# Stick-breaking attention weights: from a sum of softplus terms and one exp to sigmoid times a running product of sigmoids

## The chip, the cores and the metric

The kernel runs on one core of one Trainium2 chip. The core has a matrix engine (PE, whose weight loads the profile lists apart as PEld), a vector engine (DVE), a scalar engine for activation functions (ACT), a general engine (POOL) and DMA queues; each engine works through its own queue in order and waits for others on semaphores. PE writes only PSUM, which has eight banks of 128 x 512 fp32 words. The metric is the time of one execution on the device in microseconds (us), the median of several runs.

## The reference

The model is a decoder trunk of two layers on 512 tokens of width 1024. Every layer is an FFN with half weight, a mixer, and another FFN with half weight. The first layer's mixer is a gated linear attention (GLA), the second's is a stick-breaking attention (SB) with 16 heads of 64 channels. The change is in the SB mixer:

```
z = einsum('bhtd,bhsd->bhts', q_blk, k) * scale          # scale = 1/8
mask = s_pos[None, :] < t_pos[:, None]                    # strictly causal
sp = jnp.where(mask, jax.nn.softplus(z), 0.0)
rem = lax.cumsum(sp, axis=3, reverse=True) - sp
weights = jnp.where(mask, jnp.exp(jax.nn.log_sigmoid(z) - rem), 0.0)
o = einsum('bhts,bhsd->bhtd', weights, v)
```

So the weight of key s for query t is sigmoid(z[t,s]) times the product, over all keys u with s < u < t, of sigmoid(-z[t,u]).

## The kernel before, in words

Activations lie in SBUF transposed, channels on the partitions, as eight tiles `xs` of 128 x 512. Every large product is made from split operands: a tile `t` is cut into a rounded part `h` (fp32r, a format that PE takes in one pass) and the rest `l = t - h`, and `mm3` issues three products: h with h, l with h, h with l (line 80 is `mm`, which most of them go through). Weights come by DMA into `raw` tiles; ACT casts them to `wh` (L152), DVE subtracts to get `wl` (L153). A `Feed` object holds all weight products of the kernel as a long list of entries; a stage calls `feed.step` or `feed.halves` to put a few of those products between its own instructions. A half is a quarter of a projection for one tile (6 matmuls of 512 columns or 12 of 256).

The order of the instructions on each engine is the order in which the program writes them, as far as the framework's list scheduler doesn't move one ahead of another whose operands are late by its own model. `tc.issue_after(x)` puts an instruction behind x on the same engine. The helper `act` (L653 to L656) puts an activation behind the last load of ACT's function table, `st["tab"]`; a table load is its own ACT instruction.

The SB stage (`class SB`, its `run` from L1583) loops over s = 0 to 16. Step s makes the weights of head s (`weights_log`), and transposes and uses the weights of head s-1 (`weights`, and after each second head `values`).

- `weights_log` works in three PSUM tiles `ps_z`, numbered by `bk`: query tile 2 (384 columns of keys), query tiles 1 and 0 together (256 and 128 columns in use), query tile 3 (512 columns). For each query tile there are two matmuls, q with `kh` and q with `kl` (L1484 through `logits`). Then a mask product (also L1484, bf16, `ps_z<-negm,idb`) adds -1e30 on and above the diagonal: identity `idb` times a 128 x 128 table `negm`, once for each diagonal block. From step s = 5 on, the mask products of the first two tiles are issued ahead, in the step before (`masks`), and open the accumulation.
- From the masked logits y ACT computes |y| (L1527), exp(-|y|) and ln(1 + that) (both through L656) and relu(y) (L1530). Relu plus logarithm is softplus(y). DVE sums softplus backwards along the keys, one scan for each query tile (L1533), and subtracts: r = y - scan (L1541, reading PSUM), which is the logarithm of the weight.
- `weights` transposes r by PE in 128 x 128 blocks into three `ps_T` tiles (L1555); ACT takes exp on the way to SBUF (`wt`, through L656). Of masked places nothing remains, since exp(-1e30) is 0.
- `values` multiplies with v (L1570, `ps_oT`); ACT and DVE cut the result (L1579, L1580). The output projection (`ps_b`, through L80) starts in the last steps.
- `parts` cuts the next pair of heads' q and k tiles (L1478 on ACT, L1441 and L1464 to L1466 on DVE); its casts are put behind the relu.

PSUM tiles come from four tags: "a" 2 banks, "z" 3, "t" 2, "o" 1. `ps_z` uses "z", `ps_T` uses "t", `ps_oT` uses "o". SBUF buffers `r` are double, `l` single.

At the start of the stage a square root is taken (L578), which needs a function table of its own, and then the table with exp and ln is loaded (L651). That table serves the SB stage and then the normalisation of the FFN behind it (`rstd_wide`, Ln and Exp through L656); only after that is the table for silu loaded (L928).

Of the kernel before, what the change touches and what calls it, by code (L numbers as in the profile page):

```python
# [46 lines left out]
def decoder(ctx: ExitStack, tc: tile.TileContext, a: dict, out: bass.AP):  # L47
# [13 lines left out]
    def psum(name, tag=None):  # L61
        if tag is None:
            tag = order[turn_[0] % 8]
            turn_[0] += 1
        return pp.tile([P, T], F32, tag=tag, bufs=banks[tag], name=name)
# [580 lines left out]
            evac(ps)  # L646
        deferred.clear()

    def exp_ln_tables(after):
        with tc.issue_after(after):  # L650
            st["tab"] = nc.scalar.preload_act_table_set("natural_log_exp_and_others").ins  # L651

    def act(o, i, fn, **kw):  # L653

# [4 lines left out]
    class FFN:  # L659
# [328 lines left out]
        def run(self, between=None):  # L988
            with tc.tile_pool(name="hp", bufs=8, reuse_waits="tile") as self.hp, tc.tile_pool(
                name="tp", bufs=5, reuse_waits="tile"  # L990
            ) as self.tp:
                st["few"] = self.hp
                new_norm()
                if st["ss"] is not None:
                    if self.after_ffn:
                        exp_ln_tables(st["closed"])
                    two_halves(lambda after: sums_wide(self.tp, after))
                    rstd_wide()
                flush(self.defer)
# [24 lines left out]

    class GLA:
# [322 lines left out]
        def run(self):  # L1348
            with ExitStack() as es:
# [10 lines left out]
                stats_a("t")  # L1360
                self.gate_low()
                stats_b("t")
                exp_ln_tables(st["sqrt"])
                flush(self.defer)
                self.gate_logits()
                feed.entries(2)
# [34 lines left out]
    class SB:  # L1401
# [5 lines left out]
        AHEAD = 5  # L1407

        def __init__(self, w_in, w_out, nxt):
            self.defer, self.qk, self.hs = [], {}, []  # L1410
# [72 lines left out]
        def logits(self, o_, l_, r_, first, last=False):  # L1483
            nc.tensor.matmul(o_, l_, r_, start=first, stop=last, skip_group_check=True)  # L1484

        def mask(self, bk, ps, first):

            w = self.WID[bk]
            m0 = P if bk == 2 else w - P
            nb = (w - m0) // P  # L1490
            self.logits(
                ps[:, m0:w].rearrange("p (n s) -> p n s", n=nb),
                self.idb,
                self.negm.unsqueeze(1).to_broadcast([P, nb, P]),
                first,
                not first,
            )

        def masks(self, s):


            if self.AHEAD <= s < 16:
                for bk in (1, 2):
                    self.zs[bk] = psum("ps_z", "z")
                    self.mask(bk, self.zs[bk], True)

        def weights_log(self, p, e):

            m = self.qk[p, e, "q"]
            kh, kl = self.qk[p, e, "k"]  # L1510
            self.ys[p, e] = ys = [None] * 3
            for bk, tiles in ((1, (2,)), (2, (1, 0)), (0, (3,))):
                ahead = bk in self.zs
                ps = self.zs.pop(bk) if ahead else psum("ps_z", "z")
                w = self.WID[bk]
                for n_, i in enumerate(tiles):

                    c0, n = self.BK[i][1], max(2, i + 1) * P
                    ts_ = slice(i * P, (i + 1) * P)
                    o_, h_, l_ = ps[:, c0 : c0 + n], turns(kh)[:, 0 : n // 2], turns(kl)[:, 0 : n // 2]  # L1520
                    self.logits(o_, m[:, ts_], h_, n_ == 0 and not ahead)
                    self.logits(o_, m[:, ts_], l_, False, ahead and i == tiles[-1])
                if not ahead:
                    self.mask(bk, ps, False)
                r = self.hp.tile([P, w], F32, tag=f"r{bk}", name="r")
                l = self.hp.tile([P, w], F32, tag=f"l{bk}", bufs=1, name="l")
                nc.scalar.activation(l, ps[:, 0:w], AF.Abs)  # L1527
                act(l, l, AF.Exp, scale=-1.0)
                act(l, l, AF.Ln, bias=1.0)
                st["relu"] = nc.scalar.activation(r, ps[:, 0:w], AF.Relu).ins  # L1530
                for i in tiles:
                    c = slice(self.BK[i][1], self.BK[i][1] + (i + 1) * P)
                    nc.vector.tensor_tensor_scan(  # L1533
                        out=l[:, c][:, ::-1],
                        data0=r[:, c][:, ::-1],
                        data1=l[:, c][:, ::-1],
                        initial=0.0,
                        op0=ALU.add,
                        op1=ALU.add,
                    )  # L1540
                nc.vector.tensor_tensor(out=r, in0=ps[:, 0:w], in1=l, op=ALU.subtract)  # L1541
                ys[bk] = r
                yield

        def weights(self, p, e):
            ys = self.ys.pop((p, e))
            self.wt[p, e] = wt = []
            for bk, blocks in ((0, (0,)), (1, (1, 3)), (2, (2,))):
                ps = psum("ps_T", "t")
                w = self.TW[bk]  # L1550
                c0 = 0
                for j in blocks:
                    for i in range(j, NT):
                        yb, yc = self.BK[i]
                        nc.tensor.transpose(ps[:, c0 : c0 + P], ys[yb][:, yc + j * P : yc + (j + 1) * P], ident)  # L1555
                        c0 += P
                t = self.hp.tile([P, w], F32, tag=f"w{bk}", name="wt")
                act(t, ps[:, 0:w], AF.Exp)
                wt.append(t)
                yield  # L1560

# [21 lines left out]
        def run(self):  # L1583
            with ExitStack() as es:
# [5 lines left out]
                self.ys, self.wt, self.zs = {}, {}, {}  # L1590
# [10 lines left out]
                exp_ln_tables(st["sqrt"])  # L1601
                flush(self.defer)
                feed.step(4)

# [2 lines left out]
                for s in range(17):  # L1607
                    p, e = divmod(s, 2)
                    q, f = divmod(s - 1, 2)
                    n = steps[s]  # L1610
                    if s < 16:
                        for i, _ in enumerate(self.weights_log(p, e)):
                            if i != 1:
                                self.parts(st["relu"])
                            if i == 1:
                                k = 2 if n > 4 else 1
                                feed.halves(k)
                                n -= k
                    if s > 0:
                        for i, _ in enumerate(self.weights(q, f)):  # L1620
                            if i < 2:
                                k = min(n, n % 2 if i == 0 and n % 2 else 2)
                                feed.halves(k)
                                n -= k
                            if i == 1:
                                self.masks(s + 1)
                        feed.halves(n)
                        if f == 1:
                            self.values(q)
                    else:  # L1630
                        feed.halves(n)
# [368 lines left out]
```

## Time and profile before

| What | Value |
|---|---|
| median of 3 runs | 1758.55 us (1758.52 to 1758.58) |
| the profiled execution's own time | 1758.83 us |
| its span, first to last instruction | 1756.8 us |
| granted TensorE clock, mean | 0.999 |
| busy over the span: PE, PEld, DVE, ACT, POOL | 1744.8, 1627.8, 1508.8, 1065.0, 55.7 us |
| logits of the SB stage on PE | from 1220.5 to 1385.1 us |

How to read it: the page's first part gives the busy time of each engine. Matmuls are pipelined, so the duration that a row gives for one matmul is longer than the time until the next one starts; what a matmul costs PE is read from the distance between starts. In a timeline row stand the start in us, the duration in us, engine, line, operation, output and inputs by the program's names, shape and count, and in brackets how long the engine was idle before and who ended that. In a row of groups the two numbers behind the bar are the union of busy time in us and the mean duration of one instruction in ns; then comes the idle time before them.

### The profile page before, as it was taken

Reading aid. Unit: us, or ns where it says so; the run is one execution under the profiler, and the core shown is the slowest. Engines: PE = TensorE matmul, PEld = TensorE weight load, DVE = VectorE, ACT = ScalarE, POOL = GpSimd, SP = SyncE. Lnnn points to the kernel's source line nnn. Section 1 sums busy time; section 2 is a strip of 40 time slices with the busy share of each in tenths; the row PEclk is TensorE's granted clock in tenths of the full one; section 3 lists DMA queues with packets and bytes.
Section 4 is the critical chain, followed back from the end, with each engine's and each line's share of the span. In section 5 each row is a group of like instructions: output and inputs, shape, how many; then the busy total and the mean of one; then the engine's idle time right before and its main releaser. Section 6 shows DMA issues by size and latency. Waiting matters only on the chain.

```text
span 1756.8 us, 31456 instructions
## 1 busy us (share of the span) xinstructions
PE 1744.8 (99%) x12746; PEld 1627.8 (93%) x12746; DVE 1508.8 (86%) x2490; ACT 1065.0 (61%) x1911; POOL 55.7 (3%) x77
## 2 busy tenths in 40 slices
PE   9999999999999999999999999999999999999998
PEld 8999999889888999999989999999888889999997
DVE  8999797786888999889798988977898679998886
ACT  7556555555655555555656555655888755565555
POOL 0000000200000000000000000010000000000000
PEclk9999999999999999999999999999999999999999
DMA  5533435412123433444434344352212234434441
GB/s 168 156 110 119 130 111 146 118 56 81 57 93 100 132 109 121 120 121 127 128 101 133 103 126 129 106 133 84 85 49 73 73 96 133 123 106 121 120 137 62
DMA packets 186389, 193.16 MB, mean 110 GB/s; under 512 B 4930, under 2 KB 171124, under 8 KB 186244
## 3 DMA queue, kind: packets, MB, share of 16 engines
q1 hardware_dynamic: 177760, 175.91, 32.1%
q0 software_dynamic: 8240, 14.95, 4.7%
q8 instruction: 100, 1.64, 0.4%
q14 instruction: 45, 0.37, 0.1%
q10 hardware_dynamic: 244, 0.29, 0.0%
HBM read 175.17 MB, written 2.10 MB: 101 GB/s over the span
## 4 chain that ended last, share of the span: by engine, by line
PE 90%; DVE 6%; ACT 2%; issue 1%; DMA 1%; DVEq 0%; SPq 0%
PE ps_w L779 21%; PE ps_f L80 15%; PE ps_d L80 15%; PE ps_q L779 10%; PE ps_z L779 5%; PE ps_t L80 5%; PE ps_w L412 5%; PE ps_b L80 4%; PE ps_q L412 2%; DVE wl L153 1%; PE ps_z L1484 1%; PE ps_z L412 1%; PE ps_oT L1570 1%; PE ps_bt L80 1%; PE ps_T L1555 1%
## 5 line engine op out<-in xcount | busy, mean ns | idle before, releaser
L153 DVE TENSOR_TENSOR wl<-raw,wh 128x1024 fp32r<-128x1024 f32 x241 | 255.2, 1059 | 37.4 <-ACT wh L152 36.5
L152 ACT CAST wh<-raw 128x1024 fp32r<-128x1024 f32 x241 | 222.2, 922 | 72.2 <-PE ps_f L80 27.2
L153 DVE TENSOR_TENSOR wl<-s,wh 128x1024 fp32r<-128x1024 f32 x160 | 195.1, 1219 | 66.4 <-ACT wh L152 65.8
L779 PE MATMUL ps_w<-th,wh 128*128 128x256 f32 x864 | 238.9, 277 | 0.3 <-ACT ps_z L807 0.3
L779 PE MATMUL ps_w<-th,wl 128*128 128x256 f32 x864 | 237.6, 275 | 0.0
L779 PE MATMUL ps_w<-tl,wh 128*128 128x256 f32 x864 | 237.6, 275 | 0.0
L152 ACT CAST wh<-s 128x1024 fp32r<-128x1024 f32 x160 | 168.7, 1054 | 6.0 <-DVE s L765 6.0
L779 PEld LDWEIGHTS ps_w<-th,wh 128*128 128x128 f32 x864 | 165.8, 192 | 1.1 <-ACT ps_z L807 0.5
L80 PE MATMUL ps_f<-xh,wh 128*128 128x512 f32 x432 | 166.3, 386 | 0.0
L779 PEld LDWEIGHTS ps_w<-tl,wh 128*128 128x128 f32 x864 | 165.9, 192 | 0.0
L779 PEld LDWEIGHTS ps_w<-th,wl 128*128 128x128 f32 x864 | 165.8, 192 | 0.0
L80 PE MATMUL ps_f<-xh,wl 128*128 128x512 f32 x432 | 164.0, 380 | 0.5 <-DVE wl L153 0.5
L80 PE MATMUL ps_f<-xl,wh 128*128 128x512 f32 x432 | 163.8, 379 | 0.0
L80 PE MATMUL ps_d<-hh,wh 128*128 128x512 f32 x416 | 157.8, 379 | 0.0
L80 PE MATMUL ps_d<-hh,wl 128*128 128x512 f32 x416 | 157.7, 379 | 0.0
L80 PE MATMUL ps_d<-hl,wh 128*128 128x512 f32 x416 | 157.7, 379 | 0.0
L153 DVE TENSOR_TENSOR wl<-rawd,wh 128x1024 fp32r<-128x1024 f32 (+1 forms) x100 | 96.1, 961 | 8.9 <-ACT wh L152 8.8
L807 ACT COPY ps_z<-ps_w 128x256 f32<-128x256 f32 x72 | 26.0, 362 | 118.1 <-PE ps_w L779 117.8
L363 POOL DMA_DIRECT2D x<-d x53 | 46.0, 909 | 1549.3 <-ACT d L362 1091.4
L80 PEld LDWEIGHTS ps_f<-xh,wl 128*128 128x128 f32 x432 | 81.8, 189 | 11.4 <-DVE wl L153 0.9
L80 PEld LDWEIGHTS ps_f<-xl,wh 128*128 128x128 f32 x432 | 81.7, 189 | 11.5
L80 PEld LDWEIGHTS ps_f<-xh,wh 128*128 128x128 f32 x432 | 81.7, 189 | 10.7
(357 smaller groups left out, 5419.2 us busy)
## 6 DMA issues: line engine op xcount, KB each, us to landing
raw<-in_ffn_w_gate_dram SPq DMA_DIRECT2D x43, 1024.0 KB, 5.3
raw<-in_ffn_w_up_dram SPq DMA_DIRECT2D x43, 1024.0 KB, 5.4
rawd<-in_ffn_w_down_dram SPq DMA_DIRECT2D x84, 512.0 KB, 3.8
x<-d POOLq DMA_DIRECT2D x53, 256.0 KB, 4.8
raw<-in_gla_w_in_dram SPq DMA_DIRECT2D x12, 1024.0 KB, 5.3
raw<-in_sb_w_in_dram SPq DMA_DIRECT2D x16, 512.0 KB, 3.8
raw<-in_gla_w_out_dram SPq DMA_DIRECT2D x4, 1024.0 KB, 5.1
raw<-in_sb_w_in_dram SPq DMA_DIRECT2D x4, 1024.0 KB, 5.2
```

The lines of the kernel that those rows point to most:

```text
L80: st["pe"] = nc.tensor.matmul(ps, l, r, start=first, stop=last).ins
L152: nc.scalar.copy(h[:, k], part)
L153: nc.vector.tensor_tensor(out=l[:, k], in0=part, in1=h[:, k].bitcast(F32), op=ALU.subtract)
L363: nc.gpsimd.dma_start(xs[k], d, accum_op=ALU.add)
L412: st["pe"] = nc.tensor.matmul(ps, l_, r_, start=first and c + n == 0, stop=c == 1 and n == 2, skip_group_check=True).ins
L779: st["pe"] = nc.tensor.matmul(o, l_, r_, start=first and j + n == 0, stop=j == 3 and n == 2, skip_group_check=True).ins
L807: v["copied"] = nc.scalar.copy(z, w).ins
L1484: nc.tensor.matmul(o_, l_, r_, start=first, stop=last, skip_group_check=True)
L1555: nc.tensor.transpose(ps[:, c0 : c0 + P], ys[yb][:, yc + j * P : yc + (j + 1) * P], ident)
L1570: nc.tensor.matmul(po[e * 64 : e * 64 + 64, j * P : T], self.v[j][:, c : c + 64], self.wt[p, e][bk][:, c0 : c0 + n], start=j == 0, stop=j ...
```

## The change

The weights are computed as they stand in the last sentence on the reference, without logarithms:

- l = sigmoid(-z) for a whole `ps_z` tile (one activation), r = sigmoid(z) for each query tile by itself, without the query tile's last column (one activation each).
- The scan runs backwards over l with multiply and then add: state = state * l[u] + own[u]. `own` is a new 128 x 512 tile, zero but for an identity in its last 128 columns, so that the state is 0 until the key u = t, is set to 1 there (l[u] is multiplied into a 0), and is from then on the product of sigmoid(-z). This starts each query's product at its own diagonal and so does the masking.
- DVE multiplies r[s] by l[s+1], both in SBUF. The last column of each query tile in r is set to 0 once at the start.
- The mask products, `negm`, `idb`, the list `zs` of tiles opened ahead and `AHEAD` go. The first logit matmul opens the accumulation and the last closes it.
- The exp on the way out of the transposes becomes a copy.
- Buffers: `l` (one for each bk) and `r` (two for each bk, one for even and one for odd heads) are allocated once in the stage's pool; POOL sets `own`'s 384 zero columns and the eight zero columns of r at the start, in place of the DMA of `negm`. DVE copies the identity into `own`, in place of the copy to bf16.
- The table load at the stage's start is that with sigmoid. The FFN behind the stage loads the table with exp and ln again, behind the last sigmoid: one table load more than before.
- The casts in `parts` are put behind the last sigmoid of a tile in place of the relu.

```diff
-    def exp_ln_tables(after):
+    def tables(after, name="natural_log_exp_and_others"):
         with tc.issue_after(after):
-            st["tab"] = nc.scalar.preload_act_table_set("natural_log_exp_and_others").ins
+            st["tab"] = nc.scalar.preload_act_table_set(name).ins
...
                     if self.after_ffn:
-                        exp_ln_tables(st["closed"])
+                        tables(st["closed"])
+                    elif "sigm" in st:
+                        tables(st["sigm"])
...
-                    self.logits(o_, m[:, ts_], h_, n_ == 0 and not ahead)
-                    self.logits(o_, m[:, ts_], l_, False, ahead and i == tiles[-1])
-                if not ahead:
-                    self.mask(bk, ps, False)
-                r = self.hp.tile([P, w], F32, tag=f"r{bk}", name="r")
-                l = self.hp.tile([P, w], F32, tag=f"l{bk}", bufs=1, name="l")
-                nc.scalar.activation(l, ps[:, 0:w], AF.Abs)
-                act(l, l, AF.Exp, scale=-1.0)
-                act(l, l, AF.Ln, bias=1.0)
-                st["relu"] = nc.scalar.activation(r, ps[:, 0:w], AF.Relu).ins
+                    self.logits(o_, m[:, ts_], h_, n_ == 0)
+                    self.logits(o_, m[:, ts_], l_, False, i == tiles[-1])
+                act(l, ps[:, 0:w], AF.Sigmoid, scale=-1.0)
+                for i in tiles:
+                    c = slice(self.BK[i][1], self.BK[i][1] + (i + 1) * P - 1)
+                    act(r[:, c], ps[:, c], AF.Sigmoid)
+                st["sigm"] = st["last"]
                 for i in tiles:
                     c = slice(self.BK[i][1], self.BK[i][1] + (i + 1) * P)
                     nc.vector.tensor_tensor_scan(
                         out=l[:, c][:, ::-1],
-                        data0=r[:, c][:, ::-1],
-                        data1=l[:, c][:, ::-1],
+                        data0=l[:, c][:, ::-1],
+                        data1=self.own[:, T - (i + 1) * P :][:, ::-1],
                         initial=0.0,
-                        op0=ALU.add,
+                        op0=ALU.mult,
                         op1=ALU.add,
                     )
-                nc.vector.tensor_tensor(out=r, in0=ps[:, 0:w], in1=l, op=ALU.subtract)
+                nc.vector.tensor_tensor(out=r[:, 0 : w - 1], in0=r[:, 0 : w - 1], in1=l[:, 1:w], op=ALU.mult)
...
-                act(t, ps[:, 0:w], AF.Exp)
+                nc.scalar.copy(t, ps[:, 0:w])
...
-                self.idb = vp.tile([P, P], BF16, name="idb")
-                self.negm = vp.tile([P, P], BF16, name="negm")
-                nc.vector.tensor_copy(self.idb, ident)
-                nc.gpsimd.dma_start(self.negm, a["c_neg"])
+                self.own = vp.tile([P, T], F32, name="own")
+                nc.gpsimd.memset(self.own[:, 0 : T - P], 0.0)
+                nc.vector.tensor_copy(self.own[:, T - P : T], ident)
...
-                exp_ln_tables(st["sqrt"])
+                tables(st["sqrt"], "sigmoid_and_others")
...
-                                self.parts(st["relu"])
+                                self.parts(st["sigm"])
...
-                            if i == 1:
-                                self.masks(s + 1)
```

More of the change, by code (lines that the diff above doesn't have):

```diff
@@ L1362, in run @@
                 stats_b("t")
-                exp_ln_tables(st["sqrt"])
+                tables(st["sqrt"])
                 flush(self.defer)
@@ L1405, in decoder @@
         TW = (512, 512, 256)
-        AHEAD = 5
         def __init__(self, w_in, w_out, nxt):
@@ L1484, in logits @@
             nc.tensor.matmul(o_, l_, r_, start=first, stop=last, skip_group_check=True)
[L1486 to L1505, printed above, removed]
         def weights_log(self, p, e):
@@ L1512, in weights_log @@
             for bk, tiles in ((1, (2,)), (2, (1, 0)), (0, (3,))):
-                ahead = bk in self.zs
-                ps = self.zs.pop(bk) if ahead else psum("ps_z", "z")
+                ps = psum("ps_z", "z")
                 w = self.WID[bk]
+                r, l = self.r[bk][e], self.l[bk]
                 for n_, i in enumerate(tiles):
@@ L1589, in run @@
                 self.v = [vp.tile([P, D], F32, name=f"w{i}") for i in range(NT)]
-                self.ys, self.wt, self.zs = {}, {}, {}
+                self.ys, self.wt = {}, {}
                 self.later, self.hold = [], False
-                self.idb = vp.tile([P, P], BF16, name="idb")
-                self.negm = vp.tile([P, P], BF16, name="negm")
-                nc.vector.tensor_copy(self.idb, ident)
-                nc.gpsimd.dma_start(self.negm, a["c_neg"])
+                self.own = vp.tile([P, T], F32, name="own")
+                nc.gpsimd.memset(self.own[:, 0 : T - P], 0.0)
+                nc.vector.tensor_copy(self.own[:, T - P : T], ident)
+                self.l = [vp.tile([P, w], F32, name=f"l{bk}") for bk, w in enumerate(self.WID)]
+                self.r = []
+                for bk, w in enumerate(self.WID):
+                    self.r.append([vp.tile([P, w], F32, name=f"r{bk}{e}") for e in range(2)])
+                    for i in range(NT):
+                        if self.BK[i][0] == bk:
+                            c = self.BK[i][1] + (i + 1) * P - 1
+                            for r in self.r[bk]:
+                                nc.gpsimd.memset(r[:, c : c + 1], 0.0)
                 new_norm()
@@ L1600, in run @@
                 stats_b("t")
-                exp_ln_tables(st["sqrt"])
+                tables(st["sqrt"], "sigmoid_and_others")
                 flush(self.defer)
```

## The prediction

> **What bounds the kernel now.** I read the page first, then the busy times of the SB stage by windows, then PE's timeline there, the waits, and the groups of ACT and DVE.
>
> ```profile
> PE 1744.8 (99%) x12746; PEld 1627.8 (93%) x12746; DVE 1508.8 (86%) x2490; ACT 1065.0 (61%) x1911; POOL 55.7 (3%) x77
> PE 90%; DVE 6%; ACT 2%; issue 1%; DMA 1%; DVEq 0%; SPq 0%
> ```
>
> The second line is the chain that ended last, by engine. PE is busy 99% and carries 90% of the chain: what leaves PE's queue shortens the kernel, what leaves another engine counts only where PE waited for it. Two windows show the stage, the stretch with all heads in flight and the whole of it:
>
> ```profile
> core 0: us, PE busy (x) PEld busy (x) DVE busy (x) ACT busy (x) POOL busy (x), PEclk, DMA share, GB/s
> 1250.00:1390.00 140.00, 139.02 (x899) 115.03 (x899) 118.03 (x170) 123.56 (x253) 0.00 (x0) 1.00 0.22 69
> 1216.00:1400.00 184.00, 183.02 (x1162) 152.67 (x1161) 152.59 (x216) 156.06 (x314) 0.00 (x0) 1.00 0.24 74
> ```
>
> The reader is to see three things. PE has no room (183.02 of 184). ACT, light in the rest of the kernel, is at 88% between 1250 and 1390, so here it can be late for PE. DVE is at 84% there, and the change takes little from it. The clock is full and DMA is at a fifth to a quarter, so neither binds.
>
> **Part 1, the mask products: off the path itself.** They are counted in the row of line 1484:
>
> ```profile
> L1484 PE MATMUL ps_z<-negm,idb x48: 230/230/283, 1221.0 to 1385.1; 128*128 128x128 bf16 x32, 128*128 128x256 bf16 x16
> ```
>
> 48 of them, three for each of 16 heads. The 230 ns is not the price, since matmuls overlap; the price is how much later the following products start. There are three positions. First, the masks in line with the logits, as heads 0 to 4 have them in the first two tiles (5 heads); PE's timeline:
>
> ```profile
> 1230.19 0.33 PE L1484 MATMUL ps_z<-kl,mq 128*128 128x384 f32 x1
> 1230.36 0.23 PE L1484 MATMUL ps_z<-negm,idb 128*128 128x128 bf16 x1
> ...
> 1230.59 0.28 PE L1484 MATMUL ps_z<-kl,mq 128*128 128x256 f32 x1
> ...
> 1230.81 0.28 PE L1484 MATMUL ps_z<-kl,mq 128*128 128x256 f32 x1
> 1230.93 0.28 PE L1484 MATMUL ps_z<-negm,idb 128*128 128x256 bf16 x1
> ...
> 1231.27 0.38 PE L80 MATMUL ps_f<-xh,wl 128*128 128x512 f32 x1
> ```
>
> and the same passages in a later head, whose masks were issued ahead:
>
> ```profile
> 1285.98 0.34 PE L1484 MATMUL ps_z<-negm,idb 128*128 128x128 bf16 x2
> 1286.40 0.44 PE L1555 MATMUL ps_T<-ident,r 128*128 128x128 f32 x2
> ...
> 1286.84 0.33 PE L1484 MATMUL ps_z<-kl,mq 128*128 128x384 f32 x1
> ...
> 1287.11 0.28 PE L1484 MATMUL ps_z<-kl,mq 128*128 128x256 f32 x1
> ...
> 1287.34 0.28 PE L1484 MATMUL ps_z<-kl,mq 128*128 128x256 f32 x1
> ...
> 1287.66 0.38 PE L80 MATMUL ps_f<-xh,wl 128*128 128x512 f32 x1
> ```
>
> From `kl` to `kl` it is 1230.59 - 1230.19 = 0.40 us with the mask and 1287.11 - 1286.84 = 0.27 without: 0.13. From the last `kl` to the second weight product it is 1231.27 - 1230.81 = 0.46 with and 1287.66 - 1287.34 = 0.32 without: 0.14. Most of that is not the streaming of the mask but the product behind it, which starts its successor late after a change from bf16. Five heads at 0.27 us: 1.3 us.
>
> Second, the pair issued ahead, between weight products and transposes (heads 5 to 15, 11 heads):
>
> ```profile
> 1274.23 0.38 PE L80 MATMUL ps_f<-xl,wh 128*128 128x512 f32 x1
> 1274.45 0.34 PE L1484 MATMUL ps_z<-negm,idb 128*128 128x128 bf16 x2
> 1274.62 0.38 PE L1555 MATMUL ps_T<-ident,r 128*128 128x128 f32 x2
> ```
>
> Third, the mask of the 512-column tile, between `kl` and transposes (all heads but the first, where a weight product follows it), and a passage into transposes with no mask before it:
>
> ```profile
> 1290.26 0.38 PE L1484 MATMUL ps_z<-kl,mq 128*128 128x512 f32 x1
> 1290.47 0.23 PE L1484 MATMUL ps_z<-negm,idb 128*128 128x128 bf16 x1
> 1290.54 0.61 PE L1555 MATMUL ps_T<-ident,r 128*128 128x128 f32 x4
> ...
> 1292.07 0.38 PE L80 MATMUL ps_f<-xl,wh 128*128 128x512 f32 x1
> 1292.28 0.38 PE L1555 MATMUL ps_T<-ident,r 128*128 128x128 f32 x2
> ```
>
> Without a mask the transposes start 1292.28 - 1292.07 = 0.21 us behind a 512-column product. With the pair it is 1274.62 - 1274.23 = 0.39, with the single mask 1290.54 - 1290.26 = 0.28. So 0.18 for the pair and 0.07 for the single one: 11 x 0.18 = 2.0, 15 x 0.07 = 1.05, and 0.13 for the first head as in the first position. Sum: 1.3 + 2.0 + 1.05 + 0.13 = **4.4 us** (rounded down). Nothing covers it; PE goes straight on to the next product.
>
> **Part 2, ACT's chain.** These groups of the stage (1205 to 1402) are Exp and Ln on SBUF, and Relu from PSUM as the measure for a sigmoid:
>
> ```profile
> L656 ACT ACTIVATE l<-l 128x384 f32<-128x384 f32 x64 | 33.0, 528 | 0.2
> L656 ACT ACTIVATE l<-l 128x512 f32<-128x512 f32 x32 | 20.7, 648 | 0.0
> L1530 ACT ACTIVATE r<-ps_z 128x384 f32<-128x384 f32 x32 | 15.7, 490 | 0.0
> ```
>
> Exp and Ln go: 33.0 + 20.7 = 53.7 us. Abs becomes sigmoid(-z) on the same tile, Relu becomes sigmoid(z); whether a sigmoid takes as long as these no row shows, but exp and relu lie within 40 ns of each other here, so I take the same. Splitting the middle tile adds one instruction a head: between nothing and 0.49 us (the 384-column row), so at most 8 us. ACT's 156 us in 1216 to 1400 fall to about 102 to 110, some 60%. By itself that is worth nothing; it is worth what PE waited for ACT. The waits in the stage (1210 to 1400), of PE's weight loads:
>
> ```profile
> PEld ps_T L1555 <- ACT wt L656: 1.1, 3, 0.6
> PEld ps_b L80 <- DVE r L1541: 0.7, 1, 0.7
> PEld ps_b L80 <- ACT w L1426: 0.5, 1, 0.5
> ```
>
> Together 2.3 us. One of them is the stall in the rows above at 1285.98: the transposes come 0.42 us behind the first mask of the pair, where 1274.62 - 1274.45 = 0.17 is the undisturbed distance. It waits for an exp `wt` that frees the `ps_T` bank, at the end of an ACT backlog. The DVE row is the last head: its weights r hang on abs, exp, ln, scan. All three have ACT's chain behind them, and that chain loses two of four steps. I take **2.0 us**, near the whole, since ACT will have 40% free; the bounds are 0 (DVE takes ACT's place as the late one) and 2.3.
>
> **Part 3, DVE.** The scans stay, the subtraction becomes a product of two SBUF tiles, one column shorter:
>
> ```profile
> L1533 DVE TENSOR_TENSOR_SCAN l<-r,l 128x512 f32<-128x512 f32 x16 | 19.5, 1219 | 4.6 <-ACT l L656 4.5
> L1533 DVE TENSOR_TENSOR_SCAN l<-r,l 128x128 f32<-128x128 f32 x16 | 6.4, 399 | 0.0
> L1541 DVE TENSOR_TENSOR r<-ps_z,l 128x512 f32<-128x512 f32 x16 | 11.0, 691 | 1.0
> L536 DVE TENSOR_TENSOR ss<-ss,sq 128x512 f32<-128x512 f32 x7 | 4.8, 681 | 0.0
> ```
>
> The last row, from behind the stage, has two SBUF inputs: 681 ns against 691 with PSUM, so the product costs what the subtraction did. `ps_z` is free once ACT has read it, earlier than before, as DVE no longer reads it. A scan with multiply and add instead of add and add has no row; I take it as unchanged, the slower case is a rival. Worth 0 either way while DVE stays below PE.
>
> **Part 4, tables and the start.** One table load more, behind the last sigmoid:
>
> ```profile
> L651 ACT ACT_TABLE_LOAD  x3: 1283/1283/1283, 346.2 to 1205.8; - x3
> 1415.21 1.05 ACT L152 CAST wh<-raw 128x1024 fp32r<-128x1024 f32 x1 [7.15 <-PE ps_b L80]
> ...
> 1434.56 0.63 ACT L656 ACTIVATE R<-v 128x512 f32<-128x512 f32 x1
> L1101 POOL MEMSET w<- 128x512 f32 x1 | 1.4, 1355 | 0.0
> ```
>
> 1.28 us on ACT. Queued behind it can be casts of weights (L152), for which DVE and then PE wait; the FFN's Ln, the last row but one, needs it only at 1434.56. ACT idles 7.15 us ahead of 1415.21, and the casts there wait for PE, not for ACT. I take 0; the most it can cost is its own 1.28. [...]
>
> On POOL one DMA issue makes way for nine memsets; by the last row the largest (384 columns) takes about a microsecond. Nothing is queued behind them until the next FFN, and the first multiplication that needs them waits for a head's logits and sigmoids anyway. Worth 0.
>
> **The sum.** 1758.83 (the profiled execution) - 4.4 - 2.0 = 1752.4. The runs' median is 0.28 lower than that execution, so **1752.1 us**, 6.4 us or 0.36% faster. No change means within 0.2%, 3.5 us, about what a measurement of this kernel can tell.
>
> **Rivals.**
> *Masks only.* ACT's relief is not felt, since DVE, still at 84%, is now the late one and PE loses the same 2.0 us to it. For it: DVE has only 16% to spare, and one of the three waits is for DVE. Against it: the other two are for ACT directly, and the idle time ahead of the 512-column scans (4.6 us) ended with ACT (4.5), so DVE itself was fed late. Time 1758.55 - 4.4 = 1754.1.
> *The saving comes smaller than 3.5 us.* The list scheduler places transposes in more and smaller groups once r is ready earlier by its model; each change of format delays the next product as measured above, 0.13 us or so. Some 20 more changes cost 2.6 us, or the table load lands in front of a cast for 1.3. With masks only, 1755.4 to 1756.7.
> *Larger.* If a mask ahead of transposes gave back as much as one ahead of products, 0.27 for a pair and 0.13 for a single one, that would be 11 x 0.09 + 15 x 0.06 = 1.9 us more: 1750.2. The rows of the transposes speak against it.
> *Slower: DVE becomes the bound through the scan.* The scan's pace is (1219 - 399) / 384 = 2.14 ns an element. If a product in the recurrence takes longer than a sum, 1280 elements a head over 16 heads pay. DVE has 184 - 152.6 = 31 us of room, less the 6 us that PE gives up: 25 us, or 1.2 ns an element. Above that PE waits: at double the pace (+2.14 ns, 44 us) DVE is 19 us over, and the time is 1752.1 + 19 = 1771. It decides from about 1.5 ns an element, where the excess eats the gain. [...] No run here shows a scan with a product.
>
> **How the numbers follow.** My forecast 0.62, masks only 0.15, larger 0.08, smaller than 3.5 us 0.10, slower 0.05. The range goes from the larger case with a little margin, 1749.5, to the middle of the smaller case, 1756.0; it leaves out half of the latter, the slower one, and a little at the low end. Faster by over 0.2%: 0.62 + 0.15 + 0.08 = 0.85, less 0.02 for a masks-only case that loses more: 0.83. Within 0.2%: 0.12. Slower: 0.05.
>
> **What would show each step.** Right: in the changed profile no bf16 matmul among the logits; transposes 0.21 us behind the 512-column product before them everywhere; ACT near 60% and DVE still near 84 to 88% in the stage; no wait of PE for `wt` or `r` over 0.2 us; sigmoid rows at 0.49 and 0.61 us, scans at 1.22. The stage, from the first logit matmul to the last `ps_oT`, should be 6 us shorter, and everything behind it shifted by the same amount. Wrong: scans over 1.8 us; waits of PE for DVE l or r in every head; a stage shorter by 6 us with the gain lost behind it at the table load; or ACT as busy as before.

## The result and the profile after

The changed kernel takes 1751.95 us (median of six runs, 1751.57 to 1753.74) against 1758.54 us before (six runs, 1758.42 to 1760.37): a ratio of 0.9963, with a 95% interval from 0.9950 to 0.9976. That is 6.6 us less, where 6.4 were forecast. A second set of runs (e11 below) gave 1751.66 us and a ratio of 0.9961 (0.9948 to 0.9975). The profiled execution took 1752.18 us, its span is 1750.2 us, its granted clock 0.999.

First the page's busy times and its chain by engine:

```profile
PE 1740.0 (99%) x12698; PEld 1628.1 (93%) x12698; DVE 1507.0 (86%) x2490; ACT 1026.3 (59%) x1832; POOL 55.8 (3%) x85
PE 95%; DVE 4%; ACT 1%; issue 0%; DVEq 0%
```

PE has 48 instructions fewer, the mask products, and now carries 95% of the chain instead of 90%. DVE has as many instructions as before and 1.8 us less work. ACT lost 79 instructions and 38.7 us. The same two windows of the SB stage as before:

```profile
1250.00:1390.00 140.00, 139.79 (x886) 119.13 (x885) 117.61 (x171) 94.23 (x189) 0.00 (x0) 1.00 0.22 68
1216.00:1400.00 184.00, 183.76 (x1143) 157.44 (x1142) 155.63 (x225) 121.90 (x241) 0.00 (x0) 1.00 0.24 75
```

The columns are the window, its length, then the busy time of PE, PEld, DVE, ACT and POOL, the clock, the DMA share and GB/s. Between 1250 and 1390 PE now lacks 0.21 us of being busy throughout (0.98 before). ACT fell from 88% to 67%. DVE stays at 84%. What is left of the waits of PE and its weight loads in the stage (1210 to 1400) for another engine, in all:

```profile
PEld ps_b L80 <- ACT w L1426: 0.6, 1, 0.6
PEld ps_T L1531 <- ACT wt L1534: 0.4, 1, 0.4
PE ps_b L80 <- ACT w L1426: 0.2, 1, 0.2
```

The columns are who waited for what, us in all, how often, and the longest. The first and the last are the same place seen from the load and from the product.

Where the time went can be read from the first logit product and the last `ps_oT` of the two kernels. From the view by line, before and then after:

```profile
L1484 PE MATMUL ps_z<-kh,mq x64: 272/356/483, 1220.7 to 1384.6; 128*128 128x256 f32 x32, 128*128 128x384 f32 x16, 128*128 128x512 f32 x16
L1570 PE MATMUL ps_oT<-wt,w x128: 272/432/643, 1251.4 to 1399.2; 128*64 128x512 f32 x32, 128*64 128x384 f32 x32, 128*64 128x256 f32 x32, 128*64 128x128 f32 x32
```

```profile
L1484 PE MATMUL ps_z<-kh,mq x64: 272/301/430, 1221.0 to 1379.4; 128*128 128x256 f32 x32, 128*128 128x384 f32 x16, 128*128 128x512 f32 x16
L1546 PE MATMUL ps_oT<-wt,w x128: 272/433/644, 1250.8 to 1393.3; 128*64 128x512 f32 x32, 128*64 128x384 f32 x32, 128*64 128x256 f32 x32, 128*64 128x128 f32 x32
```

Behind the colon stand the shortest, median and longest duration in ns, then the first and the last start in us. The stage ran from 1220.7 to 1399.2, that is 178.5 us; it now runs from 1221.0 to 1393.3, that is 172.3 us. So 6.2 us of the 6.6 lie in the stage itself. The rest is small and lies outside it: in these two profiles the stage starts 0.3 us later, and some 0.7 us are gained behind it. The SB groups of the changed kernel (1205 to 1402), for ACT and DVE:

```profile
L656 ACT ACTIVATE l<-ps_z 128x384 f32<-128x384 f32 x32 | 15.8, 493 | 5.8 <-PE ps_z L1484 5.5
L656 ACT ACTIVATE r<-ps_z 128x511 f32<-128x511 f32 x16 | 9.7, 604 | 0.0
L1509 DVE TENSOR_TENSOR_SCAN l<-l,own 128x512 f32<-128x512 f32 x16 | 19.4, 1215 | 0.0
L1509 DVE TENSOR_TENSOR_SCAN l<-l,own 128x128 f32<-128x128 f32 x16 | 6.5, 406 | 0.0
L1517 DVE TENSOR_TENSOR r<-r,l 128x511 f32<-128x511 f32 x16 | 11.0, 690 | 1.2
```

A sigmoid takes what an abs or a relu took (0.49 us at 384 columns), the scan with a product what the scan with a sum took (1215 ns against 1219), the product what the subtraction took (690 against 691). And the matmuls at two of the places where masks stood, from PE's timeline:

```profile
1365.72 0.33 PE L1484 MATMUL ps_z<-kl,mq 128*128 128x384 f32 x1
...
1365.99 0.28 PE L1484 MATMUL ps_z<-kl,mq 128*128 128x256 f32 x1
...
1379.64 0.38 PE L1484 MATMUL ps_z<-kl,mq 128*128 128x512 f32 x1
1379.86 0.60 PE L1531 MATMUL ps_T<-ident,r 128*128 128x128 f32 x4
```

From `kl` to `kl` it is 0.27 us, and the transposes start 0.22 us behind the 512-column product: the undisturbed distances of the prediction.

### The profile page after: what moved, and what is told of

The parts are those of the page before. It is cut to its first block, busy times and chain, and to the rows that moved or that the text cites. A ratio compares the mean times of both kernels' runs of the same rounds, so it can differ in the third digit from the quotient of the medians.

```text
span 1750.2 us, 31332 instructions
## 1 busy us (share of the span) xinstructions
PE 1740.0 (99%) x12698; PEld 1628.1 (93%) x12698; DVE 1507.0 (86%) x2490; ACT 1026.3 (59%) x1832; POOL 55.8 (3%) x85
## 4 chain that ended last, share of the span: by engine, by line
PE 95%; DVE 4%; ACT 1%; issue 0%; DVEq 0%
PE ps_w L779 22%; PE ps_f L80 16%; PE ps_d L80 16%; PE ps_q L779 11%; PE ps_z L779 6%; PE ps_w L412 5%; PE ps_t L80 5%; PE ps_b L80 4%; PE ps_q L412 2%; PE ps_z L412 1%; PE ps_z L1484 1%; PE ps_oT L1546 1%; PE ps_T L1531 1%; PE ps_bt L80 1%; PE ps_S L80 1%; PE ps_o L80 1%
```

## The experiments

The theory: PE's path loses 4.4 us of mask products, and some 2 us in which PE waited for ACT. The first rival: masks only, because DVE takes ACT's place as the late engine. The second: DVE, with a scan that could have been slower, is close to binding. Times are medians; the ratio is to the kernel before, timed on the same chip (1758.30 to 1758.55 us).

**e1, the old chain without its masks.** The kernel before, with the mask products left out, so that its weights are not masked:

```diff
-                    self.logits(o_, m[:, ts_], h_, n_ == 0 and not ahead)
-                    self.logits(o_, m[:, ts_], l_, False, ahead and i == tiles[-1])
-                if not ahead:
-                    self.mask(bk, ps, False)
+                    self.logits(o_, m[:, ts_], h_, n_ == 0)
+                    self.logits(o_, m[:, ts_], l_, False, i == tiles[-1])
...
-                            if i == 1:
-                                self.masks(s + 1)
```

> The kernel before without its mask products (so later keys are not masked and the output is not the reference's); the log chain on ACT stays. Theory (two separate gains: 4.4 us of mask products on PE, about 2 us of waits for ACT): 1758.5 - 4.4 = 1754.1 us, and PE's waits for ACT in the stage stay at about 2 us. Rival 1 (the masks carried it all, their place in the queue made the waits): 1752 us, as the changed kernel. Rival 2 (the masks lay in time that PE waited anyway, the gain came from ACT): 1757 us or more, with longer waits for ACT.

**e2, the new chain with the old masks.** The mask products are back at their old places, adding zeros (a table of 0 instead of -1e30):

```diff
+            if self.AHEAD <= s < 16:
+                for bk in (1, 2):
+                    self.zs[bk] = psum("ps_z", "z")
+                    self.mask(bk, self.zs[bk], True)
...
-                    self.logits(o_, m[:, ts_], h_, n_ == 0)
-                    self.logits(o_, m[:, ts_], l_, False, i == tiles[-1])
+                    self.logits(o_, m[:, ts_], h_, n_ == 0 and not ahead)
+                    self.logits(o_, m[:, ts_], l_, False, ahead and i == tiles[-1])
+                if not ahead:
+                    self.mask(bk, ps, False)
...
+                nc.gpsimd.memset(self.negm, 0.0)
```

> The changed kernel with the 48 mask products back in their old three positions, with a table of zeros, so that they add nothing. Theory: 1752.0 + 4.4 = 1756.4 us, and the waits of PE for ACT stay as short as in the changed kernel. Rival 1 (masks carried it all): 1758.5 us. Rival 2 (the gain came from ACT): 1752 to 1754 us.

e1 took 1754.41 us (ratio 0.9978, 0.9969 to 0.9987), e2 1755.86 us (0.9985, 0.9977 to 0.9994). With 1758.36 before (same chip) and 1751.95 after (the first set of runs, with 1758.54 before), the masks are worth 3.95 us on the old chain and 3.9 on the new one, and the chain is worth 2.5 in both cases. Both terms exist: the runs of e1 and e2 (1754.22 to 1757.24) all lie below those of the kernel before and above those of the changed one, so "masks only" is out. Whether the two simply add up, the whole times can't tell; the stage can, and the section on the prediction comes to that. The waits of PE's weight loads in e1 show what ACT's old chain costs once the masks are gone:

```profile
PEld ps_T L1552 <- ACT wt L656: 3.2, 4, 1.1
PEld ps_b L80 <- DVE r L1538: 0.7, 1, 0.7
PEld ps_b L80 <- ACT w L1426: 0.5, 1, 0.5
```

In the kernel before these were 1.1, 0.7 and 0.5 us. Without masks PE reaches the transposes sooner, finds that `wt` has not yet left the bank, and waits 3.2 us there.

**e3, ACT's old load in the new chain.** Two copies of l on itself, between the sigmoid and the scan, in place of exp and ln:

```diff
                 act(l, ps[:, 0:w], AF.Sigmoid, scale=-1.0)
+                act(l, l, AF.Copy)
+                act(l, l, AF.Copy)
```

> The changed kernel with two more copies of l onto itself on ACT behind each sigmoid(-z), where exp and ln stood: the same chain length and nearly the same ACT load as before (about 54 us more). Theory: the waits of PE for ACT come back, 1752.0 + 2 = 1754 us. Rival (the 2 us came from something else, such as DVE not reading PSUM or the order of the queue): 1752 us.

It took 1755.00 us (0.9982, 0.9973 to 0.9991), 3.05 more than the changed kernel, and PE waits as in e1:

```profile
PEld ps_T L1533 <- ACT wt L1536: 3.2, 4, 1.2
```

So ACT's time alone brings the chain's share back, and half a microsecond more. DVE's product still reads only SBUF here, so that its subtraction read PSUM was not what cost the time. What e3 leaves open is how: because the scan gets l later, or because the copies `wt` stand further back in ACT's queue.

**e4, the same load beside the chain.** Two copies of the zero tile `own` into a tile that nobody reads, behind the sigmoids:

```diff
                 st["sigm"] = st["last"]
+                for _ in range(2):
+                    act(self.junk[:, 0:w], self.own[:, 0:w], AF.Copy)
```

> The changed kernel with the same two more ACT copies of each tile's width, but behind the sigmoids and into a scratch tile, so that the chain to the weights is as short as in the changed kernel and only ACT's load is back (about 54 us more). If ACT's backlog makes PE wait (my reading of the wait for wt): 1754 us, as with the copies in the chain. If it is the length of the chain from logits to weights: 1752 us.

It took 1769.37 us (1.0065, 1.0051 to 1.0079), which no theory gave, and the cause lies in the experiment. ACT's timeline and PE's waits:

```profile
1217.87 4.85 ACT L656 ACTIVATE junk<-own 128x512 bf16<-128x512 f32 x8
```

```profile
PE ps_oT L1548 <- ACT wt L1536: 5.7, 6, 1.9
```

The copies depend on nothing in the loop, so the list scheduler pulled them forward in bulk, eight in a row here. They stood ahead of work that PE needed. e4 does not measure what it was meant to.

**e5, the same load, held in its place.** The copies now read `ps`, and each is put behind the tile's last sigmoid:

```diff
                 st["sigm"] = st["last"]
+                with tc.issue_after(st["sigm"]):
+                    for _ in range(2):
+                        nc.scalar.copy(self.junk[:, 0:w], ps[:, 0:w])
```

> The changed kernel with two more ACT copies of each ps_z tile to a scratch tile, this time bound behind the sigmoids of that tile (they read the logits and follow the last sigmoid), so that they can't be drawn forward in a bulk as the free copies were. ACT's load is as before (about 50 us more), the chain from logits to weights stays short. If backlog on ACT makes PE wait: about 1755 us, as with the copies in the chain (1755.0). If the length of the chain does: 1752 us.

It took 1754.29 us (0.9975, 0.9966 to 0.9985): 2.3 of e3's 3.05 us come although the copies no longer stand between a tile's sigmoid and its scan. DVE's rows bear that out: idle time of the scans that ended with l is 10.2 us in e3, 1.0 in e5 and 1.8 in the changed kernel. The largest wait of PE is again the one for `wt`:

```profile
PEld ps_T L1534 <- ACT wt L1537: 3.3, 3, 1.2
```

So most of the chain's worth is the queue ahead of the copies `wt`; up to 0.7 us may be the latency of l, a difference that lies inside the intervals.

**e6 and e7, DVE's room.** One and two more scans of 512 columns for each head, on tiles that nobody reads, behind the last product:

```diff
                 ys[bk] = r
+                for _ in range(1 if bk == 0 else 0):      # e7: 2
+                    with tc.issue_after(made):            # made: the product of L1517
+                        nc.vector.tensor_tensor_scan(
+                            out=self.junk, data0=self.own, data1=self.own, initial=0.0, op0=ALU.mult, op1=ALU.add
+                        )
```

> The changed kernel with one more 512-column scan on DVE for each head, to a scratch tile, bound behind the head's last multiplication: 16 x 1.2 = 19.4 us more DVE in the stage, 175 of 178 us. Theory (PE waits for DVE only when DVE has no room left): 1752 us, at most 1 us more. Rival (DVE at 84% already decides at single places, so each more microsecond comes through in part): 1756 us or more.

> The same with two more scans for each head: 38.9 us more DVE, 194.5 us of work in a stage of 178. Theory: DVE is the bound and PE waits for the excess, 1752 + 17 = 1769 us. If DVE's work of the stage can run on behind it, where DVE is at 68%, less: 1760 us.

e7, with 32 scans of 1.22 us (39 us more for DVE), took 1769.85 us (1.0066, 1.0051 to 1.0081), close to what was expected, but in part by luck. Its stage, measured as above, takes 190.6 us, 18.3 more than that of the changed kernel. PE is idle in it for 12.4 us (0.24 in the changed kernel), where 17 us of waiting had been expected, and the largest waits are for ACT's `wt`, 11.1 us for the weight loads. The other 6 us are PE's busy time, 178.2 against 172.1, at a mean clock of 0.97. e6, with 19.5 us more, took 1754.82 us (0.9979, 0.9969 to 0.9988), where the theory had seen no loss: 2.9 us are missing. The window of e6, and its waits:

```profile
1250.00:1390.00 140.00, 138.76 (x884) 118.53 (x883) 133.79 (x189) 93.81 (x191) 0.00 (x0) 1.00 0.23 72
```

```profile
PEld ps_T L1538 <- ACT wt L1541: 3.4, 3, 1.6
```

DVE is at 96%, ACT at 67%, and yet PE waits for ACT. ACT's timeline at one of these three waits, and PE's:

```profile
1291.34 0.59 ACT L656 ACTIVATE r<-ps_z 128x511 f32<-128x511 f32 x1
...
1294.45 1.26 ACT L1478 CAST kh<-n 64x512 fp32r<-64x512 f32 x2 [2.51 <-DVE n L1451]
1295.73 1.07 ACT L1541 COPY wt<-ps_T 128x512 f32<-128x512 f32 x2
```

```profile
1296.37 0.44 PE L1538 MATMUL ps_T<-ident,r 128*128 128x128 f32 x2 [0.84 <-ACT wt L1541]
```

ACT was idle for 2.51 us. At the head of its queue stood a cast of the next heads' k, which waits for `n` from DVE; behind it stood the copies that free PE's transpose banks. At the longest of the waits it is the same with a cast of q: ACT is idle for 3.17 us until 1240.26, and PE, 1.21 us, until 1242.18. A late DVE thus appears as PE waiting for an idle ACT.

**e8, two more table loads at the stage's end.** Behind the load of the exp and ln table, the sigmoid table and the first one once more, each with a one-column activation that needs the table before it:

```diff
                         tables(st["sigm"])
+                        y = sp.tile([P, 1], F32, tag="ry", bufs=2, name="y")
+                        act(y, gT[:, 50:51], AF.Exp)
+                        tables(st["last"], "sigmoid_and_others")
+                        act(y, gT[:, 50:51], AF.Sigmoid)
+                        tables(st["last"])
```

> [...] Theory (the switch lies in ACT's idle time): 1752 us, no difference. [...]

```profile
1381.39 1.28 ACT L651 ACT_TABLE_LOAD   x1
1382.68 0.59 ACT L1539 COPY wt<-ps_T 128x512 f32<-128x512 f32 x1
1383.17 0.21 ACT L656 ACTIVATE y<-gT 128x1 f32<-128x1 f32 x1
1383.39 1.28 ACT L651 ACT_TABLE_LOAD   x1
1384.68 0.20 ACT L656 ACTIVATE y<-gT 128x1 f32<-128x1 f32 x1
```

It took 1752.68 us (0.9965, 0.9952 to 0.9977); one of its six runs took 5176.78 us, for which the profile of another run shows no reason. Its stage takes 172.3 us, as in the changed kernel, and the 0.7 us of the medians lie inside the intervals. No cost of the loads shows at this place. The rows of ACT's timeline show a load of 1.28 us, started 0.01 us after the activation before it ended, and the next instruction 1.29 us after the load's start.

**e9 and e10, the casts moved.** If the casts block the copies, they should go behind one. e9 is e6, and e10 the changed kernel, with those casts of `parts` that stood behind a head's last sigmoid put behind the second copy `wt` of the step. The casts behind the sigmoids of a head's first tile stay where they were. e11 is the changed kernel again, for comparison on the same chip:

```diff
-                nc.scalar.copy(t, ps[:, 0:w])
+                st["wt"] = nc.scalar.copy(t, ps[:, 0:w]).ins
...
-                            if i != 1:
+                            if i == 0 or i == 2 and s == 0:
                                 self.parts(st["sigm"])
...
                         for i, _ in enumerate(self.weights(q, f)):
+                            if i == 1 and s < 16:
+                                self.parts(st["wt"])
```

> The kernel with one more scan for each head, and in it the casts of q and k (L1478 on ACT, which wait for DVE's n) put behind the second copy of wt of their step instead of behind the sigmoids. If the 2.9 us of that scan came because a cast that waits for DVE stands ahead of the copies of wt in ACT's queue: most of it goes, 1752 to 1753 us. If DVE's load itself makes PE wait: still 1754.8 us. A cost of the move would be waits of PE for kh, kl or mq ahead of logits.

> The changed kernel itself with the casts moved in the same way. Only one wait for wt of 0.4 us is left in its profile, so at most 0.2 to 0.4 us are to be had: 1751.6 us; slower if the casts now come late for the logits.

> The changed kernel once more, unaltered, on the same chip and with as many rounds as the two beside it: 1752 us, and the base for both.

e9 took 1760.82 us (1.0013, 1.0005 to 1.0022), 6 us more than e6, where 2 to 3 less had been expected. Its ACT timeline and its longest wait of PE show why:

```profile
1356.70 0.58 ACT L1541 COPY wt<-ps_T 128x512 f32<-128x512 f32 x1
...
1361.49 1.26 ACT L1478 CAST kh<-n 64x512 fp32r<-64x512 f32 x2 [4.21 <-DVE n L1451]
1362.77 0.37 ACT L1541 COPY wt<-ps_T 128x256 f32<-128x256 f32 x1
```

```profile
PE ps_oT L1553 <- ACT wt L1541: 5.9, 2, 4.9
```

The moved casts now stand ahead of the third copy, and ACT stands idle in front of them for 4.21 us. The place was wrong, but the mechanism shows more clearly than in e6: a cast that waits for `n` holds up the copy behind it. Where DVE is not late, the same move does no harm: e10 took 1751.32 us (0.9958, 0.9946 to 0.9971), e11 1751.66 us (0.9961, 0.9948 to 0.9975). e10 shows no wait of PE for `wt` any more. Its 0.34 us against e11 are less than a measurement of this kernel tells apart, so it is the fastest kernel seen and not a shown improvement.

**e12, the casts off ACT.** e6 with the casts of `parts` on POOL, so that they can't stand ahead of a copy:

```diff
-                with tc.issue_after(after) if after is not None else ExitStack():
-                    nc.scalar.copy(o, i)
+                nc.gpsimd.tensor_copy(o, i)
```

> The kernel with one more scan for each head (1754.8 us), and in it the casts of q and k taken off ACT altogether: POOL, which is idle in the stage, makes them. ACT's queue then holds nothing that waits for DVE's n. If the cost of the scan came from a cast that waits for DVE ahead of the copies of wt: the waits for wt go, 1752 to 1753 us. If DVE's load itself makes PE wait: 1754.8 us or more. If POOL is slow with these casts, or slows DVE, PE waits for kh, kl or mq ahead of logits instead, and the rows of DVE get longer.

It took 1762.38 us (1.0024, 1.0014 to 1.0034). PE's largest wait for another engine in the stage, and three groups of POOL and DVE (1205 to 1402):

```profile
PE ps_T L1537 <- DVE r L1516: 5.9, 7, 1.9
```

```profile
L1477 POOL CAST mq<-n 64x512 fp32r<-64x512 f32 x16 | 19.5, 1219 | 98.1 <-DVE n L1432 97.6
L1508 DVE TENSOR_TENSOR_SCAN l<-l,own 128x512 f32<-128x512 f32 x16 | 21.1, 1320 | 0.0
L1465 DVE TENSOR_TENSOR kl<-n,kh 64x512 fp32r<-64x512 f32 x16 | 13.3, 829 | 0.4
```

The waits for `wt` fall to 0.4 us, as they should if the casts in ACT's queue caused them; ACT's load fell as well (98 against 119 us between 1216 and 1400), which e12 doesn't keep apart. But POOL takes 1.22 us for a cast of q that ACT did in 0.62, and DVE's own rows grow (the scan from 1215 to 1320 ns, the subtraction of kl from 682 in the changed kernel to 829). DVE is then truly late and PE waits for its r. Neither e9 nor e12 won the 2.9 us back, so the cause is read from the timelines of e6 and e9, and what e6 would cost with nothing blocked stays open.

## Why the prediction was right, and where it was off

**The masks, 4.4 us.** The prices held at the two places shown (0.27 and 0.22 us between starts). Two profiles of the changed kernel (the first and e11) start the stage 1.2 us apart and yet both take 172.3 us for it, so the stage tells more than the whole time. From the first logit product to the last `ps_oT` (1220.6 to 1395.9 in e1, 1220.3 to 1396.8 in e2), with PE's busy time in that window and the rest, in which PE is idle:

| Kernel | stage, us | PE busy, us | PE idle, us |
|---|---|---|---|
| before | 178.5 | 177.52 | 0.98 |
| e1, old chain, no masks | 175.3 | 173.00 | 2.30 |
| e2, new chain, masks | 176.5 | 176.36 | 0.14 |
| changed | 172.3 | 172.06 | 0.24 |

PE's busy time falls by 4.5 us when the masks leave the old chain and by 4.3 when they leave the new one: the sum of prices is about right. (The chain, too, takes 1.2 and 0.9 us off the busy time; how was not traced.) "Nothing covers it" is right only with the new chain, where the stage gets 4.2 us shorter. With the old one PE's idle time grows by 1.3 us, and the stage gains 3.2.

**ACT's chain, 2.0 us with an upper bound of 2.3.** With the masks in place the new chain shortens the stage by 2.0 us (178.5 to 176.5), as forecast. Without them it shortens it by 3.0 (175.3 to 172.3), more than the bound: PE's weight loads wait 4.4 us in e1 (3.2, 0.7 and 0.5), where they waited 2.3 before. The size of each term thus depends on which goes first: 2.0 for the chain and then 4.2 for the masks, or 3.2 for the masks and then 3.0 for the chain, 6.2 in both. The prediction took the masks at the price that they have when PE waits for nothing, and the chain at the waits seen with the masks in place. These two belong together, which it didn't argue, so the closeness of its sum has some luck in it. By medians of the whole time (3.9 to 3.95 and 2.5) this doesn't show, since the intervals of these ratios are about 0.0009 to either side, 1.6 us.

**ACT's load.** Forecast were 46 to 54 us less and some 60%; it became 34 us less (121.90 against 156.06) and 66% in the same window, 38.7 on the page. Neighbouring instructions of ACT overlap in the rows, and the prediction added up rows:

```profile
1380.06 0.60 ACT L656 ACTIVATE l<-ps_z 128x512 f32<-128x512 f32 x1 [0.42 <-PE ps_z L1484]
1380.55 0.59 ACT L656 ACTIVATE r<-ps_z 128x511 f32<-128x511 f32 x1
1381.03 0.60 ACT L1534 COPY wt<-ps_T 128x512 f32<-128x512 f32 x1
1381.64 1.28 ACT L651 ACT_TABLE_LOAD   x1
1382.93 0.58 ACT L1534 COPY wt<-ps_T 128x512 f32<-128x512 f32 x1
```

Rows of 0.60 and 0.59 us start 0.49 and 0.48 us before the next, so each adds 0.11 us less than its duration. Added up over all groups of ACT, the busy times are 1180.6 us before and 1130.0 after, 50.6 less, within the forecast; the union on the page fell by 38.7. The misreading cost nothing here, since the time hung on the waits and not on ACT's busy time.

**The waits, none for `wt` or `r` over 0.2 us.** One `wt` of 0.4 us stayed, 19 us into the stage. The wait for `w`, 0.6 us, stayed too; that sign didn't name it, but the prediction counted it among the waits that ACT's relief removes. ACT's timeline there:

```profile
1367.88 0.57 ACT L656 ACTIVATE r<-ps_z 128x255 f32<-128x255 f32 x2
1368.29 0.89 ACT L1426 ACTIVATE w<-ps_t,r 128x256 f32<-128x256 f32 x2
1369.01 1.10 ACT L152 CAST wh<-raw 128x1024 fp32r<-128x1024 f32 x1
```

`w` stands behind the sigmoids in the queue, where it stood behind exp and ln before; PE's next product starts at 1369.23. Fewer instructions ahead are not none.

**DVE, 0 us.** Right for this change: scan, product and share stayed as they were. That the scan's pace would stay was an assumption of the prediction, which had no row of a scan with a product; the rows after bear it out: (1215 - 406) / 384 = 2.11 ns an element, with sums 2.14. What failed is a rival's threshold, 25 us of room on DVE: 19.5 us more already cost 2.9 us (e6), and 39 us cost 17.9 (e7), of which 12 are waits of PE. The busy share over the stage overstated the room, since what counts is when `n` and r arrive, and a queue of ACT hangs on `n` too.

**Table load and start, 0 us.** Right: the load stands at 1381.64, and two more cost nothing (e8). The 0.3 us that the stage starts later, and the 0.7 gained behind it, were not forecast, and neither is shown to come from the change. The stage's start differs by 1.2 us between two profiles of the changed kernel (1221.0 and 1222.2 in e11). Behind the stage it is 357.6 us in the one profile of the kernel before and 356.6 in e1, which still has the old chain. The profile before has one short wait in the next FFN of PE's products that no other has:

```profile
PE ps_w L779 <- ACT ps_z L807: 0.3, 1, 0.3
```

It may account for part of the 0.7.

## What to carry to other kernels

When a change removes work from the bound engine and also what makes that engine wait, the gains of the two parts, each made alone (3.2 and 2.0 us here), need not add up to the whole (6.2): without the work the engine arrives sooner and waits longer (4.4 us in e1, 2.3 before). A wait seen beside the work is therefore no upper bound for what its removal brings once the work is gone. Add the work's full price and the waits of the trace that has the work (4.2 and 2.0), or what the work brings alone and the waits of a trace without it (3.2 and 3.0), but don't mix them. When the profile says "waits for ACT" and ACT was idle just before, look at the instruction at the head of its queue and at what that waits for: in e6 that was DVE's `n`, with ACT idle for 2.51 us, and DVE was the late engine. Room on an engine off the path is measured by adding work to it; the busy share gives only an upper bound (here 25 us on DVE, of which 19.5 already cost 2.9).

## What the runs showed of the hardware that was not expected

- In the two kernels in which PE stalls longest, its granted clock is lower as well: in e7 PE waits up to 4.3 us at a time, in e9 up to 4.9, and the clock between 1250 and 1390 is 0.96 and 0.98, while it is 1.00 in the changed kernel, with waits up to 0.2 us. Over the whole stage PE's busy time is 172.06 us in the changed kernel (clock 1.00), 175.25 in e9 (0.98) and 178.17 in e7 (0.97), for the same products, so the busy time grows about as the clock falls. Why the clock is lower there was not tested. The window of e7:

```profile
1250.00:1390.00 140.00, 131.22 (x819) 109.95 (x817) 136.20 (x186) 88.86 (x182) 0.00 (x0) 0.96 0.22 68
```

- In the kernel before, a bf16 product of 128 columns cost 0.13 us ahead of an fp32r product and 0.07 ahead of a transpose (the prediction's rows). Transposes of 32-bit tiles start at the undisturbed distance, 0.22 us behind a 512-column product, but the first product behind them starts its successor late, as the one behind a bf16 product does: after 0.30 us instead of 0.22. That lateness is there with or without a mask ahead of the transposes (0.30 us from 1290.90 to 1291.20 and from 1292.64 to 1292.94 in the kernel before), which fits the lower price of a mask at that place. The rows that follow the four transposes shown for the changed kernel:

```profile
1380.21 0.46 PE L80 MATMUL ps_b<-oh,wh 128*128 128x512 f32 x1
1380.51 0.38 PE L80 MATMUL ps_b<-oh,wl 128*128 128x512 f32 x1
1380.73 0.38 PE L80 MATMUL ps_b<-ol,wh 128*128 128x512 f32 x1
```

- With POOL casting at the same time DVE's rows are longer in e12 than in e6, by 9% for the 512-column scan (1216 to 1320 ns) and 22% for the subtraction of kl (680 to 829).
- A memset of 128 x 384 on POOL took 0.42 us, where about 1 us had been estimated from another row.
